# A two-block layer on one Trainium2 core: more subtractions on GpSimd, later gates, residual pieces further behind their loads

## The chip, the cores and the metric

One core of a Trainium2 chip (trn2) runs the whole program in one launch. The metric is device time in microseconds (us), the median of three runs. Five engines work side by side, each through its own queue in order: TensorE (PE), VectorE (DVE), ScalarE (ACT), GpSimd (POOL) and SyncE (SP), which here issues DMAs.

## The reference

256 tokens of width 2048 go through two blocks in float32. The first: a layer norm, a projection into a short convolution and an 8-head mLSTM, an output projection, a residual and layer norm, and a feed-forward part with 16384 experts. The second block (a gated recurrence, an attention with forget gates, a gated MLP) lies behind the change and isn't touched. What the change touches is the expert part:

```
q = (xt @ wq).reshape(-1, PEER_HEADS, 2, PEER_HALF)
s = jnp.einsum('thpc,hpnc->thpn', q, keys)
sv, si = lax.top_k(s, PEER_TOPK)            # 16 best of 128, twice a head
...
top_s, top_j = lax.top_k(cand, PEER_TOPK)   # 16 best of 256 sums
...
gate = jax.nn.softmax(top_s.astype(jnp.float32), axis=-1)
act = jax.nn.gelu(jnp.einsum('thkd,td->thk', ue, xt))
return jnp.einsum('thk,thkd->td', (gate * act).astype(xt.dtype), ve)
```

and then `h = layernorm(ALPHA * h + ff, ln2_g, ln2_b)`, where h is itself the first layer norm's output times gain plus bias.

## The kernel before

Each float32 product is made of three products on PE in its fast format. A weight tile of 128 x 2048 is loaded in two halves into `raw`; ACT rounds a half to `wh` (L86), and another engine subtracts to get the rest, `wl` (L87): DVE, or the engine given as `lo`. The activations are split once, into hi and lo parts. `wh` and `wl` have three buffers each, `raw` five. `dense_f` (L103) is such a step: two halves, 48 matmuls where it isn't folded, and after each half a `pump()`, which lets every generator in `trailing` go on to its next `yield`; so one step is two yields of each. `drain()` pumps until all are done.

The expert part doesn't gather: it computes all 16384 u products as 128 steps of 128 experts. Its stages in order of time:

- The queries: 16 steps over wq, each followed by scores against the keys. The generator `scores` then finds the 16 best of 128 for two token tiles on DVE (`top16`, L567 to L572), for every second step also the 16 best of the candidate sums (L584), and after heads 3, 5 and 7 a `decode` (L593 to L617) of four, two and two heads: bit arithmetic, and a one-hot comparison, product and sum (L614, L616, L617). wl comes from POOL from the fourth step on.
- The u steps 4 to 15 (L666, L667), whose Gelu goes to R0 (steps 0 to 3 were made earlier). Steps 4 to 7 have their wl from POOL, steps 8 to 15 from DVE. In their trailing runs `gates` (L641): after 18 yields it makes the softmax of the 16 scores (POOL, ACT, DVE), four yields later it transposes the first token tile's tables on PE into `tab` and six yields later the second's. A 1x1 copy from R0 on DVE (L646), the marker, makes it wait for step 11's Gelu.
- The u steps 16 to 127, with `gate_pair` (L683): for two tokens at a time POOL makes one-hot A (L687) and DVE weighted one-hot B (L690) from `tab`, PE multiplies them (L692), and the product scales R0 and R1.
- The values. Used experts are listed, and `fetch_v` and `fetch_w` on POOL's DMA queue gather their v rows (1 MB a tile) and weights five tiles ahead. For each tile, `cut` splits the weights into W_st and the rows into wh and wl, and `multiply` runs 12 matmuls of 512 columns for each token tile that the tile serves, into eight banks. There are 109 tiles in `order`; the loop at L994 runs over the first 102.
- In that loop the residual is brought back: `load_piece` issues on SP, after `hold` (a 1x1 copy of the tile's W into the destination, L72), 512 columns of the first norm's gain and bias (`gb`) and of its rows (`h1`, from DRAM). The affine (L1014) multiplies h1 by gb[0] and adds gb[1] in place, for both token tiles. Later the same pieces of gb take the second norm's gain and bias.

The framework that builds the program draws up the order of each engine's queue: by dependences, near the order of the program text, moved by its own estimate of when things are ready; an instruction whose data it takes to be there can move ahead of earlier text.

Of the kernel before, what the change touches and what calls it, by code (L numbers as in the profile page):

```python
# [7 lines left out]
F32 = mybir.dt.float32  # L8
# [3 lines left out]
AF = mybir.ActivationFunctionType  # L12
ALU = mybir.AluOpType
# [30 lines left out]
def body(tc, x, ln_in_g, ln_in_b, ln_in_gr, ln_in_br, w_conv, w_q, w_k, w_v, w_o, w_gate, b_gate,  # L44
# [5 lines left out]
    V, S, G, PE = nc.vector, nc.scalar, nc.gpsimd, nc.tensor  # L50
# [8 lines left out]
    def bank(tag, shape=(P, T)):  # L59
        return banks.tile(list(shape), F32, name="bank_" + tag, tag=tag, bufs=BANKS[tag])  # L60

    h1_d = dp.tile([P, 2, D], F32, name="h1_d")
# [7 lines left out]
    def hold(dst, after):  # L70

        V.tensor_copy(dst[0:1, 0:1], after[0:1, 0:1])  # L72
# [18 lines left out]
    def split_act(dst_h, dst_l, src):  # L91

        S.copy(dst_h, src)
        V.tensor_tensor(dst_l, src, dst_h.bitcast(F32), op=ALU.subtract)
# [10 lines left out]
    def drain():  # L105
        while trailing:
            pump()

    def dense_f(src, act, out=None, scale=None, lo=None, fold=True, m=P):


        ah, al, ax = act
        pair = bank("d", (P, 2, T))
        ps = pair[:, 0]
        for i, (wh, wl) in enumerate(split(src, lo)):
            wh = wh.rearrange("p (k f) -> p k f", f=m)
            wl = wl.rearrange("p (k f) -> p k f", f=m)
            for kk in range(8):
                k = i * 8 + kk
                if fold:  # L120
                    PE.matmul(pair, wh[:, kk], ax[:, :, k], start=(k == 0), stop=False, skip_group_check=True)  # L121
                else:
                    PE.matmul(ps, wh[:, kk], ah[:, k], start=(k == 0), stop=False)  # L123
                    PE.matmul(ps, wh[:, kk], al[:, k], start=False, stop=False)  # L124
                PE.matmul(ps, wl[:, kk], ah[:, k], start=False, stop=(k == 15), skip_group_check=fold)  # L125
            if i == 0:
                pump()
        pump()
        if not fold:
            return ps  # L130
        if out is None:
            out = wp.tile([P, T], F32, name="sum", bufs=2)
        if scale is None:
            S.copy(out, pair[:, 1])
            V.tensor_tensor(out, ps, out, op=ALU.add)
        else:
            S.activation(out, pair[:, 1], AF.Copy, scale=scale)
            V.scalar_tensor_tensor(out, ps, scale, out, op0=ALU.mult, op1=ALU.add)
        return out
# [171 lines left out]
    def act_tiles(pool=None, name="hx"):  # L311

        x = (pool or hp).tile([P, 2, KT, T], F32R, name=name, tag=name)
        return x[:, 0], x[:, 1], x
# [7 lines left out]
    with ExitStack() as ph:  # L322
# [5 lines left out]
        for t in range(2):  # L328
            for c in range(4):
                cs = slice(c * 512, (c + 1) * 512)  # L330
# [11 lines left out]
        for t in range(2):  # L342
            mv, rs = ln_stats(pp, res[:, t], t)
            for c in range(4):
                cs = slice(c * 512, (c + 1) * 512)
# [140 lines left out]
        for f in range(8):  # L486
            cs = dense_f(w_conv[1, f], act, pp.tile([P, T], F32, name="cs", bufs=2))
# [38 lines left out]
        for n in range(4):  # L526
            cs = slice(n * 512, (n + 1) * 512)
# [15 lines left out]
        R0 = hp.tile([P, J0, T], F32, name="R0", tag="r0")  # L543
# [3 lines left out]
    with ExitStack() as ph:  # L547
        def u_step(j, lo=None):
            return dense_f(u[j - 4], act, lo=lo, fold=j >= FOLD)


        with ExitStack() as pq:
# [86 lines left out]
            tab = hp.tile([P, 4, T], F32, name="tab")  # L639

            def gates():  # L641
                for _ in range(18):
                    yield
                sh = [P, 2, H, 16]
                gate = qp.tile(sh, F32, name="gate", bufs=1)
                V.tensor_copy(gate[0:1, 0, 0, 0:1], R0[0:1, 11, 0:1])  # L646
                G.tensor_tensor(gate, tv, tv[:, :, :, 0:1].to_broadcast(sh), op=ALU.subtract)
                S.activation(gate, gate, AF.Exp)
                gs = qp.tile([P, 2, H], F32, name="gs", bufs=1)
                V.tensor_reduce(gs, gate, axis=AX.X, op=ALU.add)  # L650
                V.reciprocal(gs, gs)
                V.tensor_tensor(gate, gate, gs.unsqueeze(3).to_broadcast(sh), op=ALU.mult)
                for t in range(2):
                    ts = slice(t * P, (t + 1) * P)
                    for _ in range(4 + 2 * t):
                        yield
                    for i, src in enumerate((ix[:, t, 0], ix[:, t, 1], gate[:, t])):
                        pi = bank("s", [P, P])
                        PE.transpose(pi, src.rearrange("p h k -> p (h k)"), ident)
                        if i < 2:  # L660
                            S.copy(tab[:, i, ts], pi)
                        else:
                            split_act(tab[:, 2, ts].bitcast(F32R), tab[:, 3, ts], pi)

            trailing.append(gates())
            for j in range(4, J0):  # L666
                S.activation(R0[:, j], u_step(j, G if j < 8 else V), AF.Gelu)  # L667
            drain()


# [5 lines left out]
        op = pg_.enter_context(tc.tile_pool(name="op", bufs=5))  # L676
# [128 lines left out]
        q = 0  # L805
# [33 lines left out]
        while any(left):  # L839
            c = max(range(3), key=lambda c: len(left[c]) / total[c])  # L840
            order.append(left[c].pop(0))
        order.insert(0, order.pop())
        ends = len(order) + 3
# [39 lines left out]
        def w_parts(r, pool, bufs):  # L883
            W = [pool.tile([P, T], F32R, name=n, bufs=bufs) for n in ("Wh", "Wl")]
            split_act(W[0], W[1], r)
            return W

        for k in range(KD):
            W = w_parts(R1[:, NJ - J0 + k], vp, 2)
# [45 lines left out]
        with ExitStack() as pn_:  # L935
            np_ = pn_.enter_context(tc.tile_pool(name="np", bufs=1))
# [3 lines left out]
            h1, gb = h1gb[:, 0], h1gb[:, 1]  # L940
# [13 lines left out]
            def cut(i, keep=None):  # L954

                fetch(i + 5)
                g, w = fetched_w[i]
                if keep:
                    W = np_.tile([P, 2, P], F32R, name="Wk", bufs=3)
                    W = [W[:, 0], W[:, 1]]  # L960
                else:
                    W = [W_st[:, i % 4, k, w] for k in range(2)]
                split_act(W[0], W[1], g)
                return i, W, split(fetched[i], keep=keep, there=True)
# [3 lines left out]
            def multiply(job, blocks_=range(4)):  # L968
                i, W, parts = job
                for n, t in enumerate(order[i][1]):  # L970
                    v_mm([w[:, n * P:(n + 1) * P] for w in W], parts, t, False, i == final[t], blocks_)
# [14 lines left out]
            def row_piece(row, c):  # L986
                return bass.AP(tensor=row.tensor, offset=row.offset + c.start, ap=[[0, P], [1, c.stop - c.start]])

            def load_piece(dst, src, after):
                hold(dst, after)  # L990
                nc.sync.dma_start(dst, src)

            jobs = []
            for i in range(ends):  # L994
                job = cut(i, keep if i in kept_ else None)
                if i in kept_:
                    jobs.append(job)
                else:
                    multiply(job)
                W = job[1][0].bitcast(F32)  # L1000
                if i == 5:
                    all_values()

                if 12 <= i < 28:
                    c = slice((i - 12) // 4 * 512, (i - 12) // 4 * 512 + 512)
                    if i % 4 == 0:
                        for q, row in enumerate((ln1_gr, ln1_br)):
                            load_piece(gb[:, q, c], row_piece(row, c), W)
                        for t in range(2):
                            load_piece(h1[:, t, c], h1_d[:, t, c], W)  # L1010
                if 16 <= i < 32:
                    c = slice((i - 16) // 4 * 512, (i - 16) // 4 * 512 + 512)
                    r, k = h1[:, i // 2 % 2, c], i % 2
                    V.tensor_tensor(r, r, gb[:, k, c], op=ALU.add if k else ALU.mult)  # L1014
                if ends - 40 <= i < ends - 24 and (i - ends) % 2 == 0:
                    k = (i - ends + 40) // 2
                    c = slice(k // 2 * 512, k // 2 * 512 + 512)
                    load_piece(gb[:, k % 2, c], row_piece((ln2_gr, ln2_br)[k % 2], c), W)
            for job in jobs:
                multiply(job)  # L1020
            stats = [np_.tile([P, 4, 6], F32, name="stats", bufs=2) for t in range(2)]
# [46 lines left out]
        with ExitStack() as pm:  # L1068
            mp = pm.enter_context(tc.tile_pool(name="mp", bufs=1))
            mh, ml, _ = act_tiles()  # L1070
# [61 lines left out]
            for h0 in range(0, H, 4):  # L1132
                f, kk, b, e, d = (mp.tile([P, 4, T], F32, name=n) for n in ("f", "kk", "b", "e", "d"))
# [7 lines left out]
                for i in range(4):  # L1141
# [17 lines left out]
                                op=ALU.mult)  # L1159
# [300 lines left out]
```

## Time and profile before

| | us |
|---|---|
| median of 3 runs | 3098.79 |
| lowest, highest | 3098.22, 3107.34 |
| profiled execution | 3105.84 |
| its span in the trace | 3104.1 |
| PE busy in it | 2990.2 (96%) |
| DVE busy | 2139.1 (69%) |
| ACT busy | 1489.4 (48%) |
| POOL busy | 861.6 (28%) |

The profiled execution is one more run, with the profiler on. Busy time counts work, not waits; where an engine works nearly all the time, the others' shares matter only where they hold it up. The page gives the mean granted clock of PE in tenths of full speed. A stretch of the trace is read with three views: windows (how busy each engine was), waits or groups of lines (what ended an engine's idle time), and the timeline (what ran in which order).

### The profile page before, as it was taken

To read this page: it belongs to the slowest core of one execution; us is meant where nothing else is said; L and a number is where in the kernel's file an instruction comes from. 1 tells how busy PE (TensorE), PEld (TensorE's weight loads), DVE (VectorE), ACT (ScalarE), POOL (GpSimd) and SP (SyncE) were. 2 spreads that over 40 slices of the span, in tenths; PEclk is the share of its full clock that TensorE was granted. 3 is DMA by queue.
4 is the path that set the end of the run, shared out by engine and by line. 5 is a ranking of instruction groups with operands and counts; after the bars stand their busy time and mean duration, and the time that the engine had idled before them with its cause. 6 is when DMAs were issued, how large, how long until landed. Compare 5 with 4: busy or idle time off the path is not lost. (4 is left out here: it accounts for less than half of the span.)

```text
span 3104.1 us, 46335 instructions
## 1 busy us (share of the span) xinstructions
PE 2990.2 (96%) x17152; PEld 2603.1 (84%) x17152; DVE 2139.1 (69%) x3940; ACT 1489.4 (48%) x2266; POOL 861.6 (28%) x833
## 2 busy tenths in 40 slices
PE   7999999879999999998899998999999999999998
PEld 6888879879999988886788777787888888888887
DVE  6466667969999998865666677655556666666444
ACT  5464454334444444444455655555445444444333
POOL 0000005616657847834566641000001000000000
PEclk9999999989999999998999999999999999999999
DMA  5455564335455597567778873444455555555554
GB/s 191 163 195 187 189 217 163 137 137 175 165 170 171 166 297 240 192 222 256 256 274 287 302 261 125 142 165 170 148 171 172 204 190 190 190 190 189 190 189 158
DMA packets 168124, 604.71 MB, mean 195 GB/s; under 512 B 20929, under 2 KB 37186, under 8 KB 153170
## 3 DMA queue, kind: packets, MB, share of 16 engines
q1 hardware_dynamic: 147874, 476.81, 45.0%
q0 software_dynamic: 20016, 124.86, 11.0%
q8 instruction: 137, 2.24, 0.3%
q14 instruction: 97, 0.79, 0.1%
HBM read 580.88 MB, written 20.71 MB: 194 GB/s over the span
## 5 line engine op out<-in xcount | busy, mean ns | idle before, releaser
L86 ACT CAST wh<-raw 128x1024 fp32r<-128x1024 f32 x808 | 847.4, 1050 | 1111.6 <-issue 360.0
L87 DVE TENSOR_TENSOR wl<-raw,wh 128x1024 fp32r<-128x1024 f32 x760 | 933.1, 1231 | 616.8 <-ACT wh L86 613.7
L125 PE MATMUL bank_d<-hx,wl 128*128 128x256 f32 x3008 | 848.2, 282 | 34.7 <-DVE wl L87 34.7
L121 PE MATMUL bank_d<-ax,wh 128*128 128x512 f32 x1984 | 697.0, 397 | 5.2 <-ACT wh L86 5.2
L125 PEld LDWEIGHTS bank_d<-hx,wl 128*128 128x128 f32 x3008 | 573.6, 191 | 35.8 <-DVE wl L87 35.5
L125 PE MATMUL bank_d<-ax,wl 128*128 128x256 f32 x1984 | 552.5, 279 | 0.0
L121 PE MATMUL bank_d<-hx,wh 128*128 128x512 f32 x1536 | 549.1, 400 | 0.0
L121 PEld LDWEIGHTS bank_d<-ax,wh 128*128 128x128 f32 x1984 | 373.7, 188 | 92.5 <-ACT wh L86 5.9
L123 PE MATMUL bank_d<-hx,wh 128*128 128x256 f32 x1472 | 418.7, 284 | 0.0
L124 PE MATMUL bank_d<-hx,wh 128*128 128x256 f32 x1472 | 417.2, 283 | 0.0
L125 PEld LDWEIGHTS bank_d<-ax,wl 128*128 128x128 f32 x1984 | 374.8, 189 | 0.2
L121 PEld LDWEIGHTS bank_d<-hx,wh 128*128 128x128 f32 x1536 | 288.4, 188 | 65.4
L123 PEld LDWEIGHTS bank_d<-hx,wh 128*128 128x128 f32 x1472 | 283.2, 192 | 0.0
L124 PEld LDWEIGHTS bank_d<-hx,wh 128*128 128x128 f32 x1472 | 283.2, 192 | 0.0
L234 POOL TENSOR_TENSOR rs<-rs_tmp,nhalf 128x1 f32<-128x1 f32 x12 | 10.8, 897 | 778.4 <-DVE rs_tmp L233 778.4
L87 DVE TENSOR_TENSOR wl<-kax,wh 128x1024 fp32r<-128x1024 f32 x136 | 165.5, 1222 | 73.8 <-ACT wh L86 68.3
L687 POOL TENSOR_SCALAR A<-iota,tab 128x128 fp32r<-128x128 f32 x256 | 162.1, 647 | 139.1 <-PE bank_s L692 120.5
L1337 POOL TENSOR_TENSOR res<-res,fin 128x512 f32<-128x512 f32 x6 | 8.0, 1341 | 660.9 <-ACT junk L926 660.9
L86 ACT CAST wh<-kax 128x1024 fp32r<-128x1024 f32 x136 | 142.7, 1052 | 89.9 <-PE bank_d L881 80.5
L690 DVE TENSOR_SCALAR B<-iota,tab 128x128 fp32r<-128x128 f32 x512 | 156.2, 352 | 12.2 <-PE bank_s L692 10.7
L87 POOL TENSOR_TENSOR wl<-raw,wh 128x1024 fp32r<-128x1024 f32 x48 | 118.4, 2468 | 84.5 <-ACT wh L86 84.5
L786 POOL TENSOR_SCALAR la<-lists 128x128 bf16<-128x128 f32 x126 | 131.6, 1057 | 35.8 <-PE bank_m L793 18.9
(566 smaller groups left out, 5121.6 us busy)
## 6 DMA issues: line engine op xcount, KB each, us to landing
raw<-in_u SPq DMA_DIRECT2D x256, 512.0 KB, 4.5
raw<-in_w_fg SPq DMA_DIRECT2D x88, 512.0 KB, 5.0
raw<-in_w_fu SPq DMA_DIRECT2D x88, 512.0 KB, 3.9
raw<-in_w_down SPq DMA_DIRECT2D x88, 512.0 KB, 4.8
raw<-in_w_out SPq DMA_DIRECT2D x64, 512.0 KB, 3.9
raw<-in_w_conv SPq DMA_DIRECT2D x48, 512.0 KB, 3.1
raw<-in_wq SPq DMA_DIRECT2D x32, 512.0 KB, 3.6
W_d<-R SPq DMA_DIRECT2D x40, 256.0 KB, 5.5
```

The costliest lines, as they stand in the source:

```text
L86: S.copy(wh, sl)
L87: (lo or V).tensor_tensor(wl, sl, wh.bitcast(F32), op=ALU.subtract)
L121: PE.matmul(pair, wh[:, kk], ax[:, :, k], start=(k == 0), stop=False, skip_group_check=True)
L123: PE.matmul(ps, wh[:, kk], ah[:, k], start=(k == 0), stop=False)
L124: PE.matmul(ps, wh[:, kk], al[:, k], start=False, stop=False)
L125: PE.matmul(ps, wl[:, kk], ah[:, k], start=False, stop=(k == 15), skip_group_check=fold)
L234: G.tensor_tensor(dst, tmp, nhalf[:, 0:n], op=ALU.pow)
L687: G.tensor_scalar(A, iota, tab[:, 0, t:t + 1], None, op0=ALU.is_equal)
L690: V.tensor_scalar(B[:, k], iota, tab[:, 1, t:t + 1], tab[:, 2 + k, t:t + 1], op0=ALU.is_equal, op1=ALU.mult)
L786: G.tensor_scalar(A, iota_l, lanes[:, j:j + 1], None, op0=ALU.is_equal)
L1337: G.tensor_tensor(r, r, fin[:, n * 512:(n + 1) * 512], op=ALU.mult)
```

## The change

Three edits:

- The u steps 8 to 12 have their wl from POOL too, nine steps rather than four. Steps 13 to 15 keep DVE.
- `gates` goes on after 22 yields rather than 18, in step 15 rather than 13, and its marker reads step 13's Gelu rather than step 11's. The transposes of both token tiles then come in `drain`, after step 15.
- A chunk of the residual takes twelve tiles rather than four. In tiles 0 to 3 one piece each is loaded (gain, bias, h1 of the first token tile, of the second); tiles 8 to 11 run one affine instruction each. Ahead of each multiplication a 1x1 instruction reads the piece of h1 and the second wl of the tile, so that the multiplication comes after both. The four chunks fill tiles 12 to 59 rather than 12 to 31. The loads of the second norm stay at tiles 62 to 76 (ends is 102; the formula is written out).

```
             def gates():
-                for _ in range(18):
+                for _ in range(22):
                     yield
...
-                V.tensor_copy(gate[0:1, 0, 0, 0:1], R0[0:1, 11, 0:1])
+                V.tensor_copy(gate[0:1, 0, 0, 0:1], R0[0:1, 13, 0:1])
...
-                S.activation(R0[:, j], u_step(j, G if j < 8 else V), AF.Gelu)
+                S.activation(R0[:, j], u_step(j, G if j < 13 else V), AF.Gelu)
...
+            def wait_both(a, b):
+
+                junk = np_.tile([1, 1], F32, name="one", bufs=2)
+                V.tensor_tensor(junk, a[0:1, 0:1], b[0:1, 0:1], op=ALU.max)
...
-                if 12 <= i < 28:
-                    c = slice((i - 12) // 4 * 512, (i - 12) // 4 * 512 + 512)
-                    if i % 4 == 0:
-                        for q, row in enumerate((ln1_gr, ln1_br)):
-                            load_piece(gb[:, q, c], row_piece(row, c), W)
-                        for t in range(2):
-                            load_piece(h1[:, t, c], h1_d[:, t, c], W)
-                if 16 <= i < 32:
-                    c = slice((i - 16) // 4 * 512, (i - 16) // 4 * 512 + 512)
-                    r, k = h1[:, i // 2 % 2, c], i % 2
-                    V.tensor_tensor(r, r, gb[:, k, c], op=ALU.add if k else ALU.mult)
...
+                c, k = (i - 12) // 12, (i - 12) % 12
+                cs = slice(c * 512, c * 512 + 512)
+                if 0 <= c < 4 and k < 4:
+                    if k < 2:
+                        load_piece(gb[:, k, cs], row_piece((ln1_gr, ln1_br)[k], cs), W)
+                    else:
+                        load_piece(h1[:, k - 2, cs], h1_d[:, k - 2, cs], W)
+                if 0 <= c < 4 and k >= 8:
+                    r, k = h1[:, k // 2 % 2, cs], k % 2
+                    if not k:
+                        wait_both(r, job[2][1][1].bitcast(F32))
+                    V.tensor_tensor(r, r, gb[:, k, cs], op=ALU.add if k else ALU.mult)
```

## Rows read from the trace of the kernel before

**Rows 1.** The page: busy us (share), instructions; PE's busy tenths in 40 slices.

```profile
PE 2990.2 (96%) x17152; PEld 2603.1 (84%) x17152; DVE 2139.1 (69%) x3940; ACT 1489.4 (48%) x2266; POOL 861.6 (28%) x833
...
PE   7999999879999999998899998999999999999998
```

**Rows 2.** Windows, table stage: us, busy (count) by engine, clock, DMA share, GB/s.

```profile
590.00:602.00 12.00, 12.00 (x103) 12.00 (x102) 12.00 (x68) 5.24 (x7) 9.62 (x4) 1.00 0.51 176
607.00:638.00 31.00, 0.18 (x2) 0.00 (x0) 30.76 (x172) 1.24 (x2) 0.00 (x0) 0.57 0.00 0
638.00:647.00 9.00, 8.29 (x56) 8.29 (x57) 4.16 (x5) 2.13 (x3) 0.00 (x0) 0.77 0.60 198
```

**Rows 3.** Waits, 560 to 720: waiting engine and line, releaser: total, times, longest.

```profile
PE bank_d L125 <- DVE wl L87: 31.5, 1, 31.5
```

**Rows 4.** Timeline of DVE behind 614: start us, us, instruction.

```profile
614.03 1.26 DVE L617 TENSOR_REDUCE ix<-oh 128x32 f32<-128x512 bf16 x2
...
633.07 0.17 DVE L598 TENSOR_SCALAR dn<-ti 128x32 uint32<-128x32 uint32 x1
...
637.44 3.49 DVE L87 TENSOR_TENSOR wl<-raw,wh 128x1024 fp32r<-128x1024 f32 x3
```

**Rows 5.** Timeline of POOL, table stage, idle time before in brackets.

```profile
596.51 2.40 POOL L87 TENSOR_TENSOR wl<-raw,wh 128x1024 fp32r<-128x1024 f32 x1 [0.48 <-ACT wh L86]
599.39 2.41 POOL L87 TENSOR_TENSOR wl<-raw,wh 128x1024 fp32r<-128x1024 f32 x1 [0.47 <-ACT wh L86]
...
684.67 4.95 POOL L687 TENSOR_SCALAR A<-iota,tab 128x128 fp32r<-128x128 f32 x5 [18.43 <-ACT tab L661]
```

**Rows 6.** Timeline of DVE, a decode of four heads beside POOL.

```profile
567.74 0.78 DVE L598 TENSOR_SCALAR dn<-ti 128x64 uint32<-128x64 uint32 x1
...
587.16 1.27 DVE L617 TENSOR_REDUCE ix<-oh 128x32 f32<-128x512 bf16 x2
```

**Rows 7.** Lines by form, DVE, 568 to 601, POOL subtracting: busy us, mean ns.

```profile
L614 DVE TENSOR_TENSOR oh<-rank,i 128x512 bf16<-128x512 bf16 x4 | 8.0, 2034 | 0.0
L584 DVE TENSOR_TENSOR cand<-sv 128x16 f32<-128x16 f32 x11 | 4.8, 490 | 0.0
L568 DVE MAX8 sv<-sc 128x8 f32<-128x128 f32 x6 | 1.5, 277 | 0.0
```

**Rows 8.** The same view, 608 to 637, POOL idle.

```profile
L614 DVE TENSOR_TENSOR oh<-rank,i 128x512 bf16<-128x512 bf16 x6 | 3.9, 682 | 0.0
L584 DVE TENSOR_TENSOR cand<-sv 128x16 f32<-128x16 f32 x20 | 2.5, 162 | 0.0
L568 DVE MAX8 sv<-sc 128x8 f32<-128x128 f32 x8 | 2.1, 278 | 0.0
```

**Rows 9.** Timeline of PE: first transposes of the tables, first gate matmuls.

```profile
683.28 0.38 PE L659 MATMUL bank_s<-ident,ix 128*128 128x128 f32 x2
...
692.57 0.64 PE L692 MATMUL bank_s<-B,A 128*128 128x256 f32 x4
```

**Rows 10.** Windows, value stage.

```profile
1440.00:1520.00 80.00, 60.44 (x235) 48.14 (x234) 45.44 (x68) 29.59 (x39) 36.35 (x29) 0.85 0.71 253
1560.00:1640.00 80.00, 80.00 (x354) 66.26 (x354) 52.24 (x60) 46.06 (x59) 50.90 (x39) 1.00 0.76 278
```

**Rows 11.** Lines, PE, 1440 to 1520: busy, mean ns, idle before and releaser.

```profile
L880 PE MATMUL bank_s<-wl,W_st 128*128 128x512 f32 x29 | 12.6, 435 | 19.6 <-DVE wl L87 19.6
```

**Rows 12.** The tile h1gb: its engine's idle time, and landing of its DMAs.

```profile
  DMA h1gb<-h_d: 20.1, 5
...
DMA to landing us min/median/max: 6.3/11.9/12.4
```

**Rows 13.** Timeline of DVE, first chunk: holds, then the affine.

```profile
1433.65 0.25 DVE L72 COPY h1gb<-W_st 1x1 f32<-1x1 f32 x3
...
1443.89 1.42 DVE L1014 TENSOR_TENSOR h1gb<-h1gb 128x512 f32<-128x512 f32 x2 [7.47 <-DMA h1gb<-h_d]
```

**Rows 14.** Windows, loads of the second norm.

```profile
1700.00:1720.00 20.00, 20.00 (x90) 16.58 (x89) 11.58 (x16) 10.83 (x14) 11.55 (x10) 1.00 0.91 324
```

More of the change, by code (lines that the diff above doesn't have):

```diff
@@ L1002, in body @@
                     all_values()
-                if 12 <= i < 28:
-                    c = slice((i - 12) // 4 * 512, (i - 12) // 4 * 512 + 512)
-                    if i % 4 == 0:
-                        for q, row in enumerate((ln1_gr, ln1_br)):
-                            load_piece(gb[:, q, c], row_piece(row, c), W)
-                        for t in range(2):
-                            load_piece(h1[:, t, c], h1_d[:, t, c], W)
-                if 16 <= i < 32:
-                    c = slice((i - 16) // 4 * 512, (i - 16) // 4 * 512 + 512)
-                    r, k = h1[:, i // 2 % 2, c], i % 2
-                    V.tensor_tensor(r, r, gb[:, k, c], op=ALU.add if k else ALU.mult)
[L1015 to L1018, printed above, removed]
+                c, k = (i - 12) // 12, (i - 12) % 12
[10 more added lines that the diff above has]
+                    V.tensor_tensor(r, r, gb[:, k, cs], op=ALU.add if k else ALU.mult)
+                if 62 <= i < 78 and i % 2 == 0:
+                    k = (i - 62) // 2
+                    cs = slice(k // 2 * 512, k // 2 * 512 + 512)
+                    load_piece(gb[:, k % 2, cs], row_piece((ln2_gr, ln2_br)[k % 2], cs), W)
             for job in jobs:
```

## The prediction

> **What bounds the kernel now.** Start with the page: TensorE (PE) is busy for 2990.2 of 3104.1 us, 96%, VectorE (DVE) for 69% [rows 1]. So a change pays only where PE stands still, or makes it stand still. Of the page's forty slices of 77.6 us PE is under 9 tenths in seven; the eighth and ninth (543 to 698 us) and the nineteenth and twentieth (1397 to 1552) are the places that the diff edits. I read each with windows (what is busy, at which clock), then waits or lines (who ended PE's idle time), then the timeline of the engine named.
>
> First place, the table stage. From 607 to 638 us PE is busy for 0.18 us while DVE is busy for 30.76 of 31 and GpSimd (POOL) does nothing; the granted clock averages 0.57, that is, it fell to its lower level, 1.2 GHz, after PE had stopped. From 638 to 647 the mean is 0.77: 9 x 0.23 = 2.1 us of work lost behind the stop [rows 2]. The view of waits says what PE stood for: one wait of 31.5 us, matmuls with wl for DVE's subtraction wl [rows 3]. DVE's timeline says why that was late: the first wl that DVE itself makes here starts at 637.44, behind sorting and decoding (L568 to L617) that ran without a break [rows 4]. u steps 4 to 7 had their wl from POOL, whose last part began at 599.39 and took 2.41; step 8 is the first that goes to DVE, behind its backlog.
>
> Second place, the value stage. 1440 to 1520 us holds 235 matmuls, 1560 to 1640, undisturbed, 354 of the same size [rows 10]: 119 too few, at 80 / 354 = 0.226 us, 26.9 us lost. PE's lines there give 19.6 us of idle time before matmuls that wait for wl [rows 11]; the rest, some 7 us, is the lower clock (mean 0.85 against 1.00). DVE in its turn stood 20.1 us, in five waits, for the DMA of a residual piece, which lands 6.3 to 12.4 us after its issue [rows 12]. The timeline shows the affine (L1014) reached 9 us after the holds that precede the loads, and 7.47 us of idle time before it [rows 13]: it stands in DVE's queue ahead of the wl of later tiles.
>
> **The change part by part, first: nine steps on POOL.** Ten half-step subtractions (steps 8 to 12) leave DVE for POOL. Steps run at two halves of 2.88 us, 5.76 us each (POOL's starts 596.51 and 599.39), and a part takes 2.41 [rows 5], so POOL keeps the pace, as it did in steps 4 to 7. PE then goes on from 607.2 for five more steps and stops, if at all, at 607.2 + 28.8 = 636.0. POOL's ten parts run from about 602.3 to 602.3 + 9 x 2.88 + 2.41 = 630.6.
>
> The cost is what POOL does to DVE meanwhile. The same instructions take DVE longer while POOL subtracts: the one-hot comparison L614 2034 ns against 682, the candidate sum L584 490 against 162 [rows 7, 8]. On a whole piece: the decode of four heads of one token tile ran from 567.74 to 587.16 + 1.27, 20.7 us, beside POOL [rows 6]; two heads of one tile, alone, took from 633.07 to 637.44, 4.37 us [rows 4], so four cost 8.7. The ratio is 2.4.
>
> The Trainium skill ("SBUF — State Buffer", section "SBUF: two separate sides") has a rule that speaks against this part: a DVE instruction with two SBUF inputs and a POOL instruction that reads SBUF take turns on a shared pair of ports, an exclusive lock that is held for the whole instruction. By that rule the loss can grow to POOL's whole time, which is rival C below; the rows agree with the lock, and they show DVE getting in between POOL's parts.
>
> DVE's backlog from 601.8 to 637.4 is 35.6 us when POOL rests. Its first 13.4 us, to 614.03 + 1.26 = 615.3 [rows 4], are two decodes of two heads (8.7 us) and 4.7 us of sorting. Beside POOL the decodes cost 20.7. The sorting costs between 4.7 (nothing lost) and 4.7 x 2.4 = 11.3; I take 8, about the middle, since its candidate sums stretch threefold and its MAX8 takes 277 ns against 278 [rows 7, 8]. So DVE gets to that mark at 601.8 + 28.7 = 630.5, just as POOL ends. The remaining 22.1 us run free, to 652.6, and one wl of 1.2 makes 653.8. PE stands from 636.0 to 653.8, 17.8 us, and the clock falls again, 2.1.
>
> Step 13 began, in effect, at 607.2 + 31.5 + 2.1 + 28.8 = 669.6; it begins now at 653.8 + 2.1 = 655.9. **Gain: 13.7 us**, not the 31.5 of the wait. Ends: no stretch at all, stop of 2.6 us and the clock perhaps kept, gain 31; everything at the threefold of L614, 9.6 us done in 28.8, gain 10; DVE held entirely, gain 0.
>
> **Second: gates held longer.** The work resumes in step 15 rather than 13, and its marker waits for step 13's Gelu rather than 11's. On DVE the marker has wl parts of the steps after it behind it, which are made about a step ahead; before, the same marker two steps earlier cost PE nothing, and the order relative to the steps is kept. On POOL the gate subtraction has only the A comparisons behind it. Later is the tail: the transposes of the first token tile moved from the first half of step 15 (683.28) to its end, half a step to a step, 2.9 to 4.1 us. They feed A on POOL, where four A are done by 684.67 + 4 x 0.99 = 688.6, and the first gate matmul runs at 692.57 [rows 5, 9]: slack 4.0. Cost between 0 and 4 us; I take 0.5, because the slack about equals the shift. The order of transposes is the framework's, and an earlier place would bring nothing: PE is full there.
>
> **Third: residual pieces.** The same 16 loads and 16 affines, now one load a tile in tiles 0 to 3 of each twelve and one affine a tile in tiles 8 to 11; eight 1x1 instructions are new, at most 0.25 us each by the 1x1 copies (three in 0.25 us [rows 13]), on a DVE that is busy 52 of 80 us [rows 10]: hidden. Each of them reads the piece and the second wl of its own tile, so that the affine can't be put ahead of that wl, and stands at least six tiles behind the load. A tile is 12 or 24 matmuls, 2.7 or 5.4 us; six are at least 16 us and mostly near 24, over the 12.4 of the longest landing. So DVE's 20.1 us go, PE's 19.6 with them, and the falls of the clock. Next late would be the fetch of rows: the loads' 16 x 256 KB over some 200 us add 21 GB/s to 278, so the DMA share goes from 0.76 to about 0.82; PE was full at a share of 0.91 [rows 10, 14]. The SP queue holds nothing else here that PE needs. The loads of the second norm stay at tiles 62 to 76, after the last affine at 59. **Gain: 25 us** of 26.9, 2 left for small waits; ends 0 (the waits stay) and 27.
>
> **Sum.** 13.7 + 25 - 0.5 = 38. The profiled execution took 3105.84 (span 3104.1, 1.7 around it), so 3067.6 beside it; it lies 7 us above the median of the three runs, 3098.79, and the forecast counts from the median: **3061 us**.
>
> **The rivals.**
> B, little contention: DVE finishes near 640 in spite of POOL, PE's first stop is 3 us and the clock holds: 31 + 25 - 0.5 = 55, **3044**. For it: in the change DVE also loses ten subtractions. Against: those were behind the backlog, and rows 7 stand.
> C, the stop only moves: POOL holds DVE's two-input work for all of its 28.8 us, the backlog ends at 666 and PE stops at 636 for as long as before: 0 + 25 - 0.5, **3074**. For it: rows 7. Against: the 0.47 us between POOL's parts [rows 5], and the instructions that don't stretch.
> D, the change doesn't do what it says at the residual: the affines still reach DVE before their loads, for instance because the order is drawn up again, and three quarters of the loss stay: 13.7 + 6 - 0.5 = 19, **3080**. Against: the six tiles are forced by data.
> E, slower: the 256 KB pieces, issued one by one beside the fetches, land later than six tiles. Then every one of the eight new instructions stands in front of wl with its wait: 8 x 7.5 us, the longest wait of rows 13, and a fall of the clock at 2 us each, 76 us in place of 26.9: +49 - 13 = +36, **3135**. It decides from a landing of about 24 us on, twice the longest seen [rows 12].
> F, C and most of D together, within 0.3%: **3093**.
>
> **Chances.** Forecast 0.55, B 0.10, C 0.14, D 0.10, F 0.07, E 0.04. The forecast's own range is 3052 to 3068. The range to hold 8 times in 10 reaches to B and D, 3044 to 3080, and leaves out E and F. Faster by more than 0.3% (9 us, about what a measurement of this kernel tells from no change): 0.89; within it 0.07; slower 0.04.
>
> **What would show it.** Right: PE's one wait near 636 falls to about 18 us, with DVE's first wl near 652 to 655; L614 stays near 2 us until 630; no DVE wait for the residual's DMA; 1440 to 1520 (earlier by the gain) with some 350 matmuls at clock 1.00; the first gate matmul 5 to 6 us after the last Gelu of the u steps. Wrong: a stop at 636 under 5 us or over 28; an idle row with the DMA of a residual piece still before the affine or the new 1x1 instruction; PE idle time before the gate matmuls.

## The result, and the profile after

The changed kernel takes 3070.18 us (median of 4 runs, 3062.94 to 3070.75) against 3099.51 for the kernel before on the same chip (4 runs, 3098.22 to 3107.34): ratio 0.9895, 95% interval 0.9873 to 0.9917. A second series gave 3067.53 (3065.29 to 3072.56) against 3101.33, ratio 0.9895 (0.9879 to 0.9912). The profiled execution took 3070.33, 35.5 less than the one before, 3105.84.

The page after, in the form of [rows 1]: busy us, share, instructions, then PE by slice. The ninth slice is again under 9 tenths; the eighth, nineteenth and twentieth now have 9. POOL is busy 39.9 us longer, some 26 of them with subtractions. DVE is busy 6.0 us longer although it gave ten subtractions away.

```profile
PE 2984.2 (97%) x17152; PEld 2598.9 (85%) x17152; DVE 2145.1 (70%) x3938; ACT 1490.1 (49%) x2266; POOL 901.5 (29%) x843
...
PE   7999999979999999999999998999999999999998
```

The table stage, as windows (us, busy and count of PE, weight load, DVE, ACT, POOL, then clock, DMA share, GB/s). Against [rows 2] PE works on beside POOL up to 636, then stands for 20 us while DVE finishes, and the clock falls as before, to a mean of 0.61.

```profile
602.00:630.00 28.00, 28.00 (x236) 28.00 (x235) 28.00 (x73) 11.58 (x15) 24.20 (x11) 1.00 0.51 181
630.00:636.00 6.00, 6.00 (x53) 6.00 (x52) 6.00 (x20) 2.38 (x3) 1.62 (x1) 1.00 0.40 139
636.00:656.00 20.00, 0.51 (x5) 0.30 (x3) 19.76 (x123) 1.33 (x2) 0.00 (x0) 0.61 0.00 0
656.00:665.00 9.00, 7.55 (x50) 7.55 (x51) 4.89 (x5) 1.41 (x2) 0.00 (x0) 0.73 0.51 175
```

PE's waits from 560 to 720 (who, for what: total, times, longest): the 31.5 us of [rows 3] are 20.9.

```profile
PE bank_d L125 <- DVE wl L87: 20.9, 1, 20.9
```

DVE's timeline there (start us, us, instruction), beside [rows 4]: the decode of heads 4 and 5 of both token tiles, done at 615.3 before, ends at 632.76 + 1.27 = 634.03; the first wl of DVE's own starts at 656.18 and not at 637.44.

```profile
605.25 0.17 DVE L598 TENSOR_SCALAR dn<-ti 128x32 uint32<-128x32 uint32 x1
...
621.87 0.65 DVE L598 TENSOR_SCALAR dn<-ti 128x32 uint32<-128x32 uint32 x1
...
632.76 1.27 DVE L617 TENSOR_REDUCE ix<-oh 128x32 f32<-128x512 bf16 x2
...
656.18 3.49 DVE L87 TENSOR_TENSOR wl<-raw,wh 128x1024 fp32r<-128x1024 f32 x3
```

The same instructions by form, DVE, 602 to 634, POOL subtracting (busy us, mean ns); for the first and the last [rows 7] have 2034 and 490, [rows 8] 682 and 162. The short L600 and L604, on 128x32 elements, take nearly as long as a POOL part, 2.40 us. POOL is held up too: three of its ten parts in a row took 2.85, 2.78 and 2.45 us, 8.22 with the pauses between them.

```profile
L614 DVE TENSOR_TENSOR oh<-rank,i 128x512 bf16<-128x512 bf16 x4 | 7.0, 1786 | 0.0
L616 DVE TENSOR_TENSOR oh<-oh,sf 128x512 bf16<-128x512 bf16 x4 | 5.9, 1519 | 0.0
L600 DVE TENSOR_SCALAR dn<-dn 128x32 uint32<-128x32 uint32 x2 | 4.7, 2366 | 0.0
L604 DVE TENSOR_TENSOR dn<-dn,dn 128x32 uint32<-128x32 uint32 x2 | 4.5, 2262 | 0.0
L584 DVE TENSOR_TENSOR cand<-sv 128x16 f32<-128x16 f32 x10 | 2.3, 275 | 0.0
```

Alone, in the view of [rows 8] of the kernel before:

```profile
L616 DVE TENSOR_TENSOR oh<-oh,sf 128x512 bf16<-128x512 bf16 x7 | 2.7, 415 | 0.0
L600 DVE TENSOR_SCALAR dn<-dn 128x32 uint32<-128x32 uint32 x3 | 0.5, 169 | 0.0
```

And POOL's timeline:

```profile
611.43 8.22 POOL L87 TENSOR_TENSOR wl<-raw,wh 128x1024 fp32r<-128x1024 f32 x3 [0.47 <-ACT wh L86]
```

The first gate matmuls, in the timeline of PE: 682.74, that is 5.6 us after the last Gelu of the u steps started (677.11 in ACT's timeline); before, 692.57 [rows 9].

```profile
682.74 0.64 PE L692 MATMUL bank_s<-B,A 128*128 128x256 f32 x4
```

The value stage in windows, the same work some 10 us earlier than in [rows 10], the first with 235 matmuls and a clock of 0.85 there:

```profile
1430.00:1510.00 80.00, 80.00 (x352) 65.52 (x351) 53.73 (x70) 46.18 (x58) 56.99 (x41) 1.00 0.83 306
1550.00:1630.00 80.00, 80.00 (x353) 65.95 (x352) 56.19 (x73) 45.22 (x57) 53.45 (x38) 1.00 0.81 285
```

DVE's waits there, 1410 to 1640: the DMA of h1gb, 20.1 us in [rows 12], is on the list no more.

```profile
DVE wl L87 <- ACT wh L86: 68.1, 34, 4.4
DVE W_st L94 <- ACT W_st L93: 3.6, 4, 1.4
```

Where the time came from can be added up by setting each PE instruction of one trace beside the same one (line, tile, rank) of the other and taking the difference of their starts. After less before: +0.5 at the start of the table stage, -10.1 behind the stop, -9.8 behind the first gate matmuls, -11.5 at 1420, -37.9 at 1520, -33.1 at 1740, -35.6 at 1800, -36.0 at the end. So the first edit gave 10.6 (0.5 to -10.1), the gates took 0.25, and the residual pieces gave 26.4, of which 4.8 were given back by 1740 and 2.4 came again; where those went was not followed up. Another 1.7 came between the gates and 1420, most of it at a branch (L976) that no edit touches. "Difference in the traces", below, is this count.

### The profile page after: what moved, and what is told of

The parts are those of the page before. It is cut to its first block, busy times and chain, and to the rows that moved or that the text cites. A ratio compares the mean times of both kernels' runs of the same rounds, so it can differ in the third digit from the quotient of the medians.

```text
span 3068.1 us, 46353 instructions
## 1 busy us (share of the span) xinstructions
PE 2984.2 (97%) x17152; PEld 2598.9 (85%) x17152; DVE 2145.1 (70%) x3938; ACT 1490.1 (49%) x2266; POOL 901.5 (29%) x843
## 5 line engine op out<-in xcount | busy, mean ns | idle before, releaser
L87 DVE TENSOR_TENSOR wl<-raw,wh 128x1024 fp32r<-128x1024 f32 x750 | 919.8, 1230 | 600.3 <-ACT wh L86 597.3
L87 POOL TENSOR_TENSOR wl<-raw,wh 128x1024 fp32r<-128x1024 f32 x58 | 144.6, 2494 | 87.2 <-ACT wh L86 87.1
L690 DVE TENSOR_SCALAR B<-iota,tab 128x128 fp32r<-128x128 f32 x512 | 156.6, 352 | 11.5 <-PE bank_s L692 9.8
```

Source lines behind the costliest of these rows:

```text
L87: (lo or V).tensor_tensor(wl, sl, wh.bitcast(F32), op=ALU.subtract)
L690: V.tensor_scalar(B[:, k], iota, tab[:, 1, t:t + 1], tab[:, 2 + k, t:t + 1], op0=ALU.is_equal, op1=ALU.mult)
```

## The experiments

**The edits alone.** Two kernels; first the two edits of the table stage without the residual's.

```
-                c, k = (i - 12) // 12, (i - 12) % 12
...
-                        wait_both(r, job[2][1][1].bitcast(F32))
...
+                if 12 <= i < 28:
+                    c = slice((i - 12) // 4 * 512, (i - 12) // 4 * 512 + 512)
...
```

> The u steps and the gates as changed, the residual as before. If the two places are independent (my theory): PE's stop at 636 us of about 21 us and the table stage about 10 us shorter, as in the changed kernel, while 1440 to 1520 keeps its loss of about 27 us; about 10 us (0.3%) under the kernel before. Rival: the residual's waits come from what the table stage leaves behind and shrink with it; then 20 us or more under it.

Measured 3091.56 us against 3101.58, ratio 0.9969 (0.9960 to 0.9979). PE's wait is that of the changed kernel, and the value stage is that of before: in the traces -10.6 in the table stage, and nothing gained in the value stage. PE's one wait between 560 and 720 is again of 20.9 us. The window of the value stage:

```profile
1430.00:1510.00 80.00, 59.79 (x232) 47.84 (x233) 45.51 (x69) 29.65 (x38) 36.19 (x29) 0.85 0.68 242
```

Then the residual's edit alone.

```
-                for _ in range(22):
+                for _ in range(18):
-                V.tensor_copy(gate[0:1, 0, 0, 0:1], R0[0:1, 13, 0:1])
+                V.tensor_copy(gate[0:1, 0, 0, 0:1], R0[0:1, 11, 0:1])
-                S.activation(R0[:, j], u_step(j, G if j < 13 else V), AF.Gelu)
+                S.activation(R0[:, j], u_step(j, G if j < 8 else V), AF.Gelu)
```

> The residual as changed, the u steps and the gates as before. My theory: the 31.5 us wait of the table stage is back, no DVE wait for a residual piece, 25 to 28 us (0.8 to 0.9%) under the kernel before. Rival: part of the 27 us needs the other edit; then under 20 us.

Measured 3077.51, ratio 0.9928 (0.9913 to 0.9942): the wait of 31.5 is there again, and the value stage gives 26.4. The two places are independent: 0.0031 and 0.0072 add up to 0.0103, the whole change gave 0.0105, each with an interval of about 0.001 to 0.002 either way. Windows of the value stage:

```profile
1440.00:1520.00 80.00, 79.99 (x352) 65.55 (x351) 53.79 (x70) 45.72 (x58) 56.52 (x40) 1.00 0.84 306
```

**The gates.** The changed kernel with the old place of the gates.

```
-                for _ in range(22):
+                for _ in range(18):
-                V.tensor_copy(gate[0:1, 0, 0, 0:1], R0[0:1, 13, 0:1])
+                V.tensor_copy(gate[0:1, 0, 0, 0:1], R0[0:1, 11, 0:1])
```

> The changed kernel with the gates at 18 yields and step 11's Gelu again. Theory: the gates' place is covered either way; within 1 us of the changed kernel in the trace, the first gate matmul at the same distance from the last u step. Rival: the earlier marker or its table load stands in the way beside POOL's parts, 2 to 5 us slower.

Measured 3067.63, ratio 0.9891 (0.9875 to 0.9908). In the traces it is 0.3 us ahead of the changed kernel behind this stage. The edit has no measurable effect.

**What POOL's subtractions cost DVE.** The changed kernel without the ten subtractions of steps 8 to 12.

```
-            (lo or V).tensor_tensor(wl, sl, wh.bitcast(F32), op=ALU.subtract)
+            if sub: (lo or V).tensor_tensor(wl, sl, wh.bitcast(F32), op=ALU.subtract)
...
-                S.activation(R0[:, j], u_step(j, G if j < 13 else V), AF.Gelu)
+                S.activation(R0[:, j], u_step(j, G if j < 13 else V, sub=not 8 <= j < 13), AF.Gelu)
```

> The changed kernel with the subtraction of steps 8 to 12 left out: wh is used in wl's place, PE does as many matmuls, POOL rests. My theory, POOL's subtractions stretch DVE's sorting and decoding: DVE's first own wl starts near 638 us rather than 656, L614 at about 0.68 us after 602, PE's stop at 636 is 2 to 4 us and the clock stays high; some 20 us under the changed kernel. Rival, the backlog itself grew (order or waits of DVE): first wl still at 650 or later, a stop of 14 us or more.

Measured 3048.25 (2 runs), ratio 0.9832 (0.9812 to 0.9851). PE's wait shrinks to 2.7 us (waits, 560 to 720), and DVE's two instructions are back near the times of [rows 8] (lines by form, 602 to 636):

```profile
PE bank_d L125 <- DVE wl L87: 2.7, 1, 2.7
```

```profile
L614 DVE TENSOR_TENSOR oh<-rank,i 128x512 bf16<-128x512 bf16 x7 | 4.5, 680 | 0.0
L584 DVE TENSOR_TENSOR cand<-sv 128x16 f32<-128x16 f32 x30 | 4.5, 189 | 0.0
```

So PE's wait is 18.2 us shorter, and in the traces the first gate matmul comes 28.5 us ahead of the kernel before, against 10.4 in the changed kernel: POOL's ten subtractions, some 25 us of POOL, cost DVE some 18 us of the 28.8 that they cover.

**Backlog moved out of the way.** The decodes of all heads are put off and run in eight pieces of two heads, one every two or three half steps of the u steps, each behind the wl made last (`last`, set in `split`); POOL subtracts only in steps 4 and 5.

```
-                            decode(t, *pieces[h])
+                            units.extend((t, pieces[h][0] + k) for k in range(0, pieces[h][1], 2))
...
-                x, s5, a, b = n
+                x, s5, a, b = n; hold(s5[:, 0], last[0].bitcast(U32))
...
+            def decodes():
+                for k, n in enumerate([5, 2, 3, 2, 3, 2, 3, 2]):
+                    for _ in range(n):
+                        yield
+                    if k == 0:
+                        units.sort()
+                    decode(*units[k], 2)
+
+            trailing.extend([decodes(), gates()])
...
-                S.activation(R0[:, j], u_step(j, G if j < 13 else V), AF.Gelu)
+                S.activation(R0[:, j], u_step(j, G if j < 6 else V), AF.Gelu)
```

> The changed kernel with the decodes of all heads put off, in eight units of two heads, each behind a wl part of a u step (a 1x1 copy from wl into the decode's first tile), and with POOL's parts for steps 4 and 5 alone. My theory: DVE then sorts beside POOL at PE's pace and decodes beside nothing, so that PE has no stop over 4 us between 590 and 660; 18 to 23 us under the changed kernel, about 3045. Rival, DVE's total is the bound and only the place of the stop moves: stops that sum to 12 us or more, under 10 us gained.

Measured 3051.85 (against 3101.58), ratio 0.9840 (0.9826 to 0.9855): it beats both kernels, and in the traces it is some 17 us ahead of the changed kernel behind this stage, just under the 18 to 23 expected. PE's waits, 560 to 720, and the window:

```profile
PE bank_d L125 <- DVE wl L87: 3.7, 3, 2.6
PE bank_s L659 <- DVE gate L652: 1.1, 1, 1.1
```

```profile
560.00:700.00 140.00, 135.23 (x1112) 134.44 (x1111) 135.46 (x461) 61.54 (x97) 48.62 (x51) 0.99 0.52 167
```

DVE is busy for 135.46 of the 140 us, and PE hardly waits for it: the decodes no longer stand ahead of the wl. But a second thing changed with their place. They now run where POOL doesn't subtract; lines of DVE by form, 601 to 700:

```profile
L614 DVE TENSOR_TENSOR oh<-rank,i 128x512 bf16<-128x512 bf16 x15 | 9.7, 685 | 0.0
```

Added up in the traces (overlaps counted once), all decodes take DVE 38 us here, 56 in the kernel before and 74 in the changed one. What the place in the queue gives and what the quiet neighbour gives, this run doesn't part.

**The two halves of the residual's edit.** It does two things: it makes the affine come after the loads have landed (twelve tiles, one load each), and it pins the affine behind the tile's wl (`wait_both`). First the spacing without the pin:

```
-                    if not k:
-                        wait_both(r, job[2][1][1].bitcast(F32))
```

> The changed kernel without the 1x1 instruction: one load a tile and affines seven tiles behind in the program's text, but nothing that ties them. Theory of the place: the planned order puts affines right behind the loads again, DVE waits 10 to 25 us for them and the value stage loses 10 us or more against the changed kernel. Rival of the burst: single loads land in time, DVE waits under 5 us, same time as the changed kernel.

Measured 3081.82, ratio 0.9936 (0.9920 to 0.9953), 16.6 us behind the changed kernel in the traces. DVE waits for the pieces again (waits of DVE, 1410 to 1640):

```profile
DVE h1gb L1019 <- DMA h1gb<-h_d: 14.2, 5, 7.9
DVE h1gb L1019 <- DMA h1gb<-in_ln_gr: 5.4, 1, 5.4
DVE W_st L94 <- ACT W_st L93: 4.4, 4, 2.2
DVE h1gb L1019 <- DMA h1gb<-in_ln_br: 1.8, 1, 1.8
```

These are 21.4 us, against 20.1 before: the distance in the text alone doesn't hide the loads. The order that the framework draws up puts the affines close behind the holds, whatever tile the text has them in; the data dependence of `wait_both` is what keeps them back. Still the stage keeps some 10 of the 26 us; why was not tested.

Then the pin with the old spacing, four loads every four tiles and sixteen affines in sixteen tiles:

```
-                c, k = (i - 12) // 12, (i - 12) % 12
...
+                if 16 <= i < 32:
+                    c = slice((i - 16) // 4 * 512, (i - 16) // 4 * 512 + 512)
+                    r, k = h1[:, i // 2 % 2, c], i % 2
+                    if not k:
+                        wait_both(r, job[2][1][1].bitcast(F32))
+                    V.tensor_tensor(r, r, gb[:, k, c], op=ALU.add if k else ALU.mult)
```

> The changed kernel with the residual's chunks four tiles apart again (four loads at once, affine four tiles behind), but with the 1x1 instruction that ties the affine behind its tile's wl. Theory, the place in DVE's queue is what counts: four tiles are some 16 us, over the 12.4 us of landing, so DVE waits for the pieces under 5 us in all and the value stage keeps over 20 of its 27 us. Rival, the burst of four loads is what counts: they land late, DVE waits over 10 us in all and over half of the 27 us is lost.

Measured 3083.41, ratio 0.9943 (0.9926 to 0.9960): DVE's wait for the pieces is gone, as expected, but only 10 of the 26 us are gained. That was not expected. In the traces 16.6 us are lost again against the changed kernel (-0.4 at 1420, +16.2 at 1520), now by PE for wh of ACT, and by ACT for gathered columns. POOL's timeline shows why those come late: between 1440 and 1530 of the kernel before a gather issue takes 0.94 to 2.0 us; seven here took 2.4 to 5.5, of which five:

```profile
1451.10 5.51 POOL L856 DMA_INDIRECT kax<-in_v,lists  x1 [1.04 <-DVE one L992]
1460.20 3.56 POOL L865 DMA_INDIRECT gw<-W_d,lists  x1 [0.30 <-issue]
...
1492.10 5.32 POOL L856 DMA_INDIRECT rows<-in_v,lists  x1 [3.19 <-DVE one L992]
1501.19 4.90 POOL L856 DMA_INDIRECT kax<-in_v,lists  x1 [0.30 <-issue]
1509.64 5.06 POOL L865 DMA_INDIRECT gw<-W_d,lists  x1 [0.30 <-issue]
```

and ACT's timeline the waits that follow:

```profile
1468.68 0.50 ACT L93 CAST W_st<-gw 128x128 fp32r<-128x128 f32 x2 [8.14 <-DMA gw<-W_d,lists]
...
1520.93 0.30 ACT L93 CAST W_st<-gw 128x128 fp32r<-128x128 f32 x1 [9.50 <-DMA gw<-W_d,lists]
```

**Loads or affines?** Two kernels. In the changed one, the four loads of a chunk at once:

```
-                if 0 <= c < 4 and k < 4:
+                if 0 <= c < 4 and k == 0:
+                    for q, row in enumerate((ln1_gr, ln1_br)):
+                        load_piece(gb[:, q, cs], row_piece(row, cs), W)
+                    for t in range(2):
+                        load_piece(h1[:, t, cs], h1_d[:, t, cs], W)
```

> The changed kernel with the four loads of a slice (two rows, two pieces of h1) all issued behind the first tile of its twelve, and not one a tile; the affines stay where the change puts them, the first eight tiles on, each pair behind the wait of line 992. Theory (what costs the four-tile version its 16 us is the affines in sixteen tiles in a row): bursts alone cost little, the value stage stays within 4 us of the changed kernel, 3066 to 3073 us, ratio 0.988 to 0.992. Rival (four loads of 256 KB at once push the gathers of the next tiles back): four bursts cost at least 8 us, 3077 us or more.

Measured 3067.83, ratio 0.9894 (0.9877 to 0.9910). From 1420 to 1640 it neither gains nor loses against the changed kernel (+4.2 at 1420, +4.5 at 1620): bursts cost nothing.

And the four-tile version without its affines and the small waits ahead of them:

```
-                    if not k:
-                        wait_both(r, job[2][1][1].bitcast(F32))
-                    V.tensor_tensor(r, r, gb[:, k, c], op=ALU.add if k else ALU.mult)
```

> The four-tile version with its sixteen affines (multiply by the row, add the row) and the eight small waits in front of them left out, so h1 keeps its raw pieces; the loads stay in bursts of four, every four tiles. Theory (the affines lengthen POOL's gather issues): the loss of 16 us beside the changed kernel goes, 3064 to 3071 us, ratio 0.987 to 0.991, and no gather issue on POOL above 2.5 us between 1450 and 1512. Rival (the bursts of loads delay the gathers): the loss stays, 3077 us or more, with ACT still waiting for gathered columns 8 to 10 us at a time.

Measured 3064.77, ratio 0.9891 (0.9875 to 0.9908). No issue is over 2 us between 1450 and 1512, and of the 16.6 us that the four-tile version loses there against the changed kernel, 3.0 are left (+0.5 to +3.5). So the affines cost the other 13.6. How they do it the two timelines say together. DVE's at one of the long issues (four-tile version, POOL's from 1501.19 to 1506.09):

```profile
1501.53 0.67 DVE L1022 TENSOR_TENSOR h1gb<-h1gb 128x512 f32<-128x512 f32 x1
1502.13 1.21 DVE L87 TENSOR_TENSOR wl<-kax,wh 128x1024 fp32r<-128x1024 f32 x1
1503.27 0.67 DVE L1022 TENSOR_TENSOR h1gb<-h1gb 128x512 f32<-128x512 f32 x1
1503.87 1.20 DVE L87 TENSOR_TENSOR wl<-kax,wh 128x1024 fp32r<-128x1024 f32 x1
1505.01 0.27 DVE L94 TENSOR_TENSOR W_st<-gw,W_st 128x128 fp32r<-128x128 f32 x1
```

Each starts before the one ahead of it has ended; the row ends at 1505.01 + 0.27 = 1505.28, and the issue 0.81 us later. Of the other six long ones four ended 0.82 or 0.83 us after such a row, the one at 1451.10 0.81 after W_st, when one-element copies followed, and one 0.81 after an affine inside a row. The changed kernel has the same rows, only further apart: 3.58 and 4.71 us in POOL's timeline, ended 0.84 and 0.82 after such rows, with time to catch up in between.

```profile
1468.19 3.58 POOL L856 DMA_INDIRECT kax<-in_v,lists  x1 [0.30 <-issue]
...
1476.69 4.71 POOL L865 DMA_INDIRECT gw<-W_d,lists  x1 [0.30 <-issue]
```

It needs no affine. The kernel before has one such issue later on, beside a row of wl and W_st alone; POOL's timeline, and the first and last of DVE's row:

```profile
1687.82 5.58 POOL L865 DMA_INDIRECT gw<-W_d,lists  x1 [1.12 <-DVE h1gb L72]
```

```profile
1687.30 1.20 DVE L87 TENSOR_TENSOR wl<-kax,wh 128x1024 fp32r<-128x1024 f32 x1
...
1691.37 1.21 DVE L87 TENSOR_TENSOR wl<-rows,wh 128x1024 fp32r<-128x1024 f32 x1
```

The row ends at 1692.58, the issue 0.82 later, at 1693.40. So it is the unbroken row that an issue waits out; the affines make rows where there were gaps.

**Cutting the row.** The four-tile version with a one-element copy behind each affine:

```
                     V.tensor_tensor(r, r, gb[:, k, c], op=ALU.add if k else ALU.mult)
+                    V.tensor_copy(np_.tile([1, 1], U32, name="brk", bufs=2), r[0:1, 0:1].bitcast(U32))
```

> The four-tile version with one more DVE instruction behind each of its sixteen affines: a copy of one element (1x1), which the queue puts behind the next wl subtraction. In the four-tile version six gather issues of POOL took 3.6 to 5.5 us, and each ended about 0.8 us after DVE's unbroken row of two-tensor instructions (wl, affine, wl, affine, wl, W_st) came to a pause or to a one-element copy. Theory (POOL cannot finish issuing a gather while such a row runs): the copies cut the rows, no issue between 1450 and 1515 lasts over 3 us, and most of the 12 us that the affines cost comes back: 3066 to 3075 us, ratio 0.988 to 0.992. Rival (the affines cost what they take of DVE, 0.67 us each): 16 copies of 0.13 us add 2 us, 3081 to 3088 us, and the long issues stay.

Measured 3075.47, ratio 0.9916 (0.9901 to 0.9931), just outside what the theory gave and well below the rival's: 3.9 of the 13.6 us came back in the traces. The queue's order put the copy behind the next wl, not behind the affine, and the issues now end there. Timeline of DVE, and of POOL beside it: the wl ahead of the copy ends at 1509.14 + 1.21 = 1510.35, the issue at 1508.21 + 2.96 = 1511.17, 0.82 later, while DVE goes on.

```profile
1508.54 0.67 DVE L1022 TENSOR_TENSOR h1gb<-h1gb 128x512 f32<-128x512 f32 x1
1509.14 1.21 DVE L87 TENSOR_TENSOR wl<-kax,wh 128x1024 fp32r<-128x1024 f32 x1
1510.28 0.13 DVE L1023 COPY brk<-h1gb 1x1 uint32<-1x1 uint32 x1
1510.34 1.20 DVE L87 TENSOR_TENSOR wl<-rows,wh 128x1024 fp32r<-128x1024 f32 x1
```

```profile
1508.21 2.96 POOL L856 DMA_INDIRECT kax<-in_v,lists  x1 [0.30 <-issue]
```

Seven of the eight longest issues ended so, 0.81 to 0.83 us after the wl ahead of a copy; one (5.58 us) ran past its first copy. So a row can be cut, but up to the copy it is still some 2 us long. What the issues between 1440 and 1530 take beyond 1.8 us each, added up, goes with the loss: 18.4 us in the four-tile version, which loses 16.6 to the changed kernel; 12.9 with the copies, which loses 12.7; 0.2 without the affines, which loses 3.0. Beyond those 3.0 that is 0.74 and 0.75 us a microsecond, in the two versions that there are. The theory's "most of the 12" was wrong, as it took the rows to be cut at the affine.

**The best version with the same copies.**

```
 # k_defer, and behind each affine
+                    V.tensor_copy(np_.tile([1, 1], U32, name="brk", bufs=2), r[0:1, 0:1].bitcast(U32))
```

> The version that puts all heads' decodes off behind the u steps (3051.85 us) with the same one-element copy behind each of the changed kernel's affines. Theory of the row: the long gather issues beside the affines go (3.58, 4.71, 3.25 and 5.52 us in that kernel), but PE waited for nothing there between 1410 and 1530, so the gain is at most 3 us: 3048 to 3054 us, ratio 0.983 to 0.985. Rival (the copies only load DVE): the issues stay, same time or up to 3 us more.

Measured 3053.90 (3046.32 to 3055.06), ratio 0.9845 (0.9832 to 0.9859). No difference from 0.9840. The expectation that the long issues would go failed: three between 1440 and 1530 took 2.98, 6.50 and 2.42 us, and the one of 6.50 ran past a copy too. PE did not wait for them, as in the changed kernel.

## Why the prediction came out as it did

**Right: what bounded the kernel, and that the two places are independent.** The edits alone gave 10.6 and 26.4 us where the prediction read 31.5 and 26.9 us of loss, and their ratios add up.

**Mis-sized: part one, 10.6 for 13.7.** PE reached the stop as worked out (636.0; 636.5 in the trace, which lies 0.5 later), and what was left of DVE's backlog behind the contended stretch took 656.18 - 634.03 = 22.15 us, predicted 22.1. The term that was off is the stretch itself: "its first 13.4 us" beside POOL took not 28.7 but about 31.7 (602.3 to 634.03), and the stop 20.9 instead of 17.8. It came out near the prediction's own low end, gain 10.

Divided among the instructions, the stretch shows two errors that partly cancel. The sorting, for which 8 us were set, took 5.7, against 5.4 alone: it lost next to nothing. The two decodes, for which 20.7 us were set, took 25.9, against 8.0 alone. The 20.7 was the price of one decode of four heads [rows 6], and two decodes of two heads aren't that: each has its own short instructions, and beside POOL a short one can cost as much as a POOL part. L600 ran from 605.78 to 608.20 beside the part that ended at 608.16. L600 and L604 together took 9.2 us in the two decodes, and less than 1 us when POOL rests.

The rule behind rival C (the Trainium skill, "SBUF — State Buffer", section "SBUF: two separate sides": two SBUF inputs on DVE against a reading POOL instruction, an exclusive lock for the whole instruction) holds in kind. Without the subtractions L614 falls from 1786 to 680 ns and the stop to 2.7 us. But DVE lost some 18 us of 28.8, not all of it; that is why the stop shrank and did not only move.

**Right: gates.** 0.5 predicted, 0.25 in the trace, 0.3 in the experiment. The shift of the transposes was given as half a step to a step, 2.9 to 4.1 us; at 5.76 us a step it would be 2.9 to 5.8, which made no difference here.

**Right in size, thin in reason: part three, 25.** The stage gained 26.4 and kept about 24. The reason given was the six tiles between load and affine and the pin. The experiments show that both are needed, each alone keeping 10 us of the 26, and that the pin does what the prediction ascribed to it: without it the queue's order puts the affines back ahead. But spreading over twelve tiles does not help by the landing time only. In the four-tile version no affine waited for a load, and 16.6 us were lost all the same, 13.6 of them by late gathers beside the affines. The prediction counted the affines' DVE time as hidden and looked for the next late thing in DMA bandwidth; it was POOL's issuing beside DVE, of which the trace of before had an example (5.58 us at 1687.82). It did not matter between 1410 and 1560, where PE waits for nothing: the twelve tiles left time to recover. That they would was not foreseen, so the right size of 25 owes something to luck.

**The total.** Beside the profile 3067.6 was forecast, and 3070.33 came: 2.7 off. That looks like the 3.1 of part one, but part three kept 1 us less than its 25 as well, and the 1.7 between the two places, which no part of the prediction holds, made up for some of it. The median of 3061 was 9 too low: 3070.18 lies 2 us outside the forecast's own 3052 to 3068, inside the range of 3044 to 3080, and nearer to rival C's 3074. The time doesn't tell the two apart, the trace does: C wanted a stop as long as before, 31.5 us, and it was 20.9. The step behind the other 6.5 is the last one, which took the gain, read from an execution 7 us above its median, off that median: the execution profiled after lies on its median, not 7 above. Later series of the kernel before had medians of 3101 to 3102. The change keeps 29 to 34 us by the medians, 35.5 by the profiles. Traces differ by up to 3 us at start-up, where all kernels have the same work, and two of the changed kernel by as much at the branch (L976) near 1400, so single runs don't tell these apart.

## What to carry to other kernels

When a stop is due to one engine's backlog, ask first whether the backlog must stand ahead of the work that the bottleneck needs: putting the decodes behind it, where the neighbour was quiet too, gave some 27 us here; handing the subtractions to a neighbour that slows the backlog gave 10.6. A wait written into the program text only helps if a data dependence holds it there, since the order is drawn up again. Price contention by a row of the same shape in the same company, by the number of instructions as well as by their size, and look for it on both engines: in the four-tile version the next late thing was the neighbour's DMA issues.

## What the runs showed of the hardware

Two things had not been expected. A gather issue of POOL, 0.9 to 2.0 us otherwise, stretched to as much as 5.6 us beside DVE's two-tensor instructions when they followed each other without a gap, with the affines and without them, and ended some 0.8 us after such a row did; in the version without affines a gap of 0.02 or 0.03 us on DVE was enough (issues of 1.78 us, 0.8 after it). A copy of one element in the row let it through in seven of eight cases; one of 5.58 us, and one of 6.50 us in the best version, ran past a copy.

The loss in POOL's company isn't a constant of the instruction: L614 took 2034 ns in one stretch and 1786 in the other, the candidate sum 490 and 275, against 682 and 162 alone. The short L600 grew most, from 169 to 2366 ns, the time of about one POOL part, and of POOL's own parts those beside L614 and L616 grew from 2.40 to 2.85 and 2.78.
